# Sums, feature combinations, squares and low halves moved from GpSimd to VectorE in a two-layer diffusion transformer

## The chip, the cores and the metric

The kernel runs on one core of a Trainium2 chip. The metric is the device time of one execution in microseconds (us); the time shown for the kernel before is the median of three runs. Five engines work side by side: TensorE (PE in the profile, with PEld for its weight loads), VectorE (DVE), ScalarE (ACT), GpSimd (POOL) and SyncE (SP), which issues the transfers here.

## The reference, cut to what matters

Two layers run over 1024 latent tokens and 256 context tokens of width 1024. Layer 0 mixes by dense grouped attention and a pooling mixer, layer 1 by windowed attention. Around every mixer and every feed-forward block stand an RMS norm, a modulation from a conditioning vector, and a second norm on the way out:

```python
mod = (silu_c @ w_mod[l] + b_mod[l])[:, None, :]
sh_m, sc_m, gt_m, sh_f, sc_f, gt_f = jnp.split(mod, 6, axis=-1)
h = rmsnorm(x, g_pre_mix[l]) * (1 + sc_m) + sh_m
x = x + gt_m * rmsnorm(mixer(h), g_post_mix[l])
h = rmsnorm(x, g_pre_ffn[l]) * (1 + sc_f) + sh_f
g, u = jnp.split(h @ w_in, 2, axis=-1)
x = x + gt_f * rmsnorm((silu(g) * u) @ w_out, g_post_ffn[l])
```

The context goes through the same with its own modulation, in layer 0 only.

## The kernel before, in words

**Precision by halves.** Matrix products are made in a 32-bit format that TensorE takes in one pass. To keep accuracy, each operand is split: ScalarE copies it to that format (the high half, names with `wh`, `hh`, `th`, `ph`), and a subtraction leaves the low half (`wl`, `hl`, `tl`, `pl`). `split` does this for activations and `wunit` for a 128x1024 piece of weights. A product is then three matmuls. The variable `wpool[0]` says how many of the 1024 columns of a weight's low half GpSimd makes; VectorE makes the rest. It is set from the constants `WP0` to `WP7`, `OUTWP0` and `OUTWP` stage by stage, and to all 1024 columns inside `pair_up`, for the units of the gate weights that are kept for later.

**Tiles.** The tokens are held with features on the partitions, in chunks of 512 latent tokens (`l0`, `l1`) and 256 context tokens (`cc`). Large tiles come from a ring of 38 buffers (`Q`), half-size ones from a ring of 19 (`S`), modulation weights from a ring of 3 (`MW`), and results of matmuls from 8 banks (`ps`).

**Norms.** `rstd` squares eight feature rows on ScalarE and adds the squares in two accumulators; before the change the first is added on VectorE and the second on GpSimd. VectorE then adds the two, TensorE sums over the partitions, ScalarE takes the root, VectorE the reciprocal, and TensorE spreads it over the partitions again. `postnorm` scales the block's output and adds it to the stream (feature rows 1, 3 and 5 of that addition on GpSimd, the others on VectorE); `prenorm` makes the split input of the next product.

**Modulation.** `mod_row` makes two of layer 0's six vectors by matmul. `mod_vec` makes the others by multiply-and-add over eight 128-row pieces of the weights: an addend with number `(k + 2c) % 4` below `pool` is scaled on ScalarE (`S_mp`) and added on GpSimd, the others are one instruction on VectorE (`S_ma`). Layer 0's vectors 2, 3 and 4 are called with `POOLC`, which is 4 before, so that all their sums go to GpSimd; the rest of the vectors use VectorE alone.

**Feed-forward by a fast product.** The gate product of chunk `l0` is made ahead of time (`ffn_gates`) while attention runs, and chunk `l1` follows in `ffn_pair` by a two-by-two fast matrix product that needs sums and differences of inputs and weights. `pair_up` leads into it: output projection's `postnorm`, `rstd`, the last kept gate units, and `prenorm_pair`, which makes for each of four feature rows four combinations of the two chunks (`S_t`) and splits five (`Q_th`, `Q_tl`). For each of the 22 units of weights, `ffn_pair` makes four combinations of weight columns (`Q_sw`), splits them (`Q_wh`, `Q_wl`; `S_wh`, `S_wl`), runs the products, adds their results (`S_v`), multiplies by the gate (`S_v` again) and splits the result (`S_act`), which goes to memory. `ffn_out` multiplies that by the output weights.

**Who sets the order.** Nothing runs as it is written. `Plan` records every instruction, gives it a cost by a table, and `layout` places the instructions by list scheduling: per engine, the ready one with the lowest priority number, subject to free buffers and to a rule that VectorE and GpSimd do not run instructions on on-chip operands at one time (`port_free`). Each engine then works through its fixed list in order. All instructions are issued from line 419, so the profile's groups are told apart by the tiles' names.

Quoted, `wunit`'s division of a low half:

```python
c = D - wpool[0]
if c:
    V.tensor_tensor(wl[:, :c], raw[:, :c], r32(wh[:, :c]), op=ALU.subtract)
if c < D:
    G.tensor_tensor(wl[:, c:], raw[:, c:], r32(wh[:, c:]), op=ALU.subtract)
```

Of the kernel before, what the change touches and what calls it, by code (L numbers as in the profile page):

```python
# [32 lines left out]
MODLATE = (2, 3, 4)  # L33
POOLE = 4
OUTM = ("0", "c")
OUTWP0 = 1024
OUTWP = 500
OUTL = False
TAILX = (1, 3, 5, 7)
WP0 = 200  # L40
WP1 = 0
WP2 = 200
WP3 = 500
WP4 = 340
WP5 = 0
WP6 = 0
REST = 1.0
WP7 = 600
SIZES = (2, 4, 4, 4, 4, 4), (2, 4, 4, 4, 4, 4), (4, 4, 4, 4, 6)
EARLY = 2  # L50
PSPL = True
POOLC = 4
SHARES = (0.9, 0.95, 0.9, 0.7)
KEPT = (5, 2), (7, 3)
POOLX = (1, 3, 5)
# [371 lines left out]
def tile_dit(  # L427
# [92 lines left out]
    def split(hi, lo, src, pool=False):  # L520
        S.activation(hi, src, AF.Copy)
        (G if pool else V).tensor_tensor(lo, src, r32(hi), op=ALU.subtract)
# [15 lines left out]
    def rstd(xf):  # L538
        n = xf.ch.n
        kk, nt = 512 // n, n // P  # L540
        accs = [None, None]
        for k in range(0, KT, kk):
            sq = st([P, kk, n], F32, "sq")
            for j in range(kk):
                S.activation(sq[:, j, :], xf.k(k + j), AF.Square)
            i = k // kk % 2
            if accs[i] is None:
                accs[i] = sq
            else:
                (G if i else V).tensor_tensor(accs[i], accs[i], sq, op=ALU.add)  # L550
        acc, other = accs
        V.tensor_tensor(acc, acc, other, op=ALU.add)
        acc = acc[:, 0, :]
        if kk > 1:
            V.tensor_tensor(acc, acc, accs[0][:, 1, :], op=ALU.add)
        ps = pst(2 * nt)
        for t in range(nt):
            T.matmul(ps[:, 2 * t:2 * t + 2], acc[:, t * P:(t + 1) * P], ones2, start=True, stop=True)
        r = small([P, 4], F32, "rs")[:, :nt]
        S.activation(r, ps[:, 0:2 * nt:2], AF.Sqrt, bias=epsc, scale=1.0 / D)  # L560
        V.reciprocal(r, r)
        rb = st([P, 4, P], F32, "rb")[:, :nt, :]
        V.tensor_copy(rb, r.unsqueeze(2).to_broadcast([P, nt, P]))
        pr = pst(n)
        for t in range(nt):
            T.transpose(pr[:, t * P:(t + 1) * P], rb[:, t, :], ident)
        return pr
# [18 lines left out]
    def prenorm_pair(xf, r, x0, l, kind):  # L586

        a = fin[:, l, 2 * kind, 0, :]  # L590
        b = mod[:, l, 3 * kind, 0, :]
        db = small([P, 4], F32, "db")
        V.tensor_tensor(db, b[:, 4:8], b[:, 0:4], op=ALU.subtract)
        for k in range(KT):
            V.scalar_tensor_tensor(xf.k(k), xf.k(k), a[:, k:k + 1], r, op0=ALU.mult, op1=ALU.mult)
        t = [(Quad("th"), Quad("tl")) for _ in range(5)]
        for k in range(4):
            lo1, hi1, lo0, hi0 = xf.k(k), xf.k(k + 4), st([P, 512], F32, "x0"), st([P, 512], F32, "x0")
            SP.dma_start(out=lo0, in_=x0[:, k, :])
            SP.dma_start(out=hi0, in_=x0[:, k + 4, :])  # L600
            bk = b[:, k + 4:k + 5]
            t1, t2, t3, t4 = (st([P, 512], F32, "t") for _ in range(4))
            G.tensor_tensor(t1, lo1, lo0, op=ALU.subtract)
            V.scalar_tensor_tensor(t2, hi1, bk, t1, op0=ALU.add, op1=ALU.subtract)
            V.scalar_tensor_tensor(t3, hi1, db[:, k:k + 1], lo1, op0=ALU.add, op1=ALU.subtract)
            V.scalar_tensor_tensor(t4, hi0, bk, t2, op0=ALU.add, op1=ALU.subtract)
            for i, f in ((1, t2), (2, t3), (0, t1), (3, t4)):
                split(t[i][0].k(k), t[i][1].k(k), f, i in (0, 2))
            S.activation(t[4][0].k(k), hi1, AF.Identity, bias=bk, scale=1.0)
            V.scalar_tensor_tensor(t[4][1].k(k), hi1, bk, r32(t[4][0].k(k)), op0=ALU.add, op1=ALU.subtract)  # L610
        return t
# [165 lines left out]
    def ffn_pair(l, t, first, hc=None):  # L777
# [3 lines left out]
        for u in range(NH):  # L781
# [5 lines left out]
            gs = qt_([P, 2, 512], F32, "gs")  # L787
            SP.dma_start(out=gs, in_=g_scr[l][:, u, :, :])
            p1, p2 = (qt_([P, 2, 512], F32, "sw") for _ in range(2))
            G.tensor_tensor(p1[:, 0, :], up[:, 0:512], up[:, 512:1024], op=ALU.add)  # L790
            G.tensor_tensor(p1[:, 1, :], p1[:, 0, :], ga[:, 0:512], op=ALU.subtract)
            G.tensor_tensor(p2[:, 0, :], ga[:, 0:512], up[:, 0:512], op=ALU.subtract)
            G.tensor_tensor(p2[:, 1, :], ga[:, 512:1024], p1[:, 1, :], op=ALU.subtract)
            s12, s34 = [(qt_([P, 2, 512], F32R, "wh"), qt_([P, 2, 512], F32R, "wl")) for _ in range(2)]
            a22 = st([P, 512], F32R, "wh"), st([P, 512], F32R, "wl")
            split(*s12, p1)
# [17 lines left out]
            def late(u=u, gs=gs, s34=s34, p5=p5, v2=v2, uu=uu, cu=cu, cg=cg, prod=prod):  # L814
                prod(p5, s34, 1, b22, False, True)
                V.tensor_tensor(cg, v2, p5, op=ALU.add)
                for ch, g, v in ((L0, gs[:, 1, :], uu), (L1, cg, cu)):
                    S.activation(g, g, AF.Silu)
                    G.tensor_tensor(v, v, g, op=ALU.mult)
                    hi, lo = st([P, 512], F32R, "act"), st([P, 512], F32R, "act")  # L820
                    split(hi, lo, v)
                    for j, o in enumerate((hi, lo)):
                        SP.dma_start(out=a_scr[l][ch][:, u, j, :], in_=r32(o))
# [736 lines left out]
```

## Time and profile before

| what | value |
|---|---|
| median of three runs | 2852.52 us (2847.48 to 2853.18) |
| the profiled execution's own time | 2850.01 us |
| its span, first to last instruction | 2848.1 us |
| mean granted TensorE clock | 0.968 |
| bytes moved | 481.08 MB, mean 169 GB/s |

The stages lie in the span about as follows: start and first projections to 100 us; layer 0's attention, pooling mixer and later modulation vectors to 400; output projections and the way into the second attention to 550; attention of `l1` with gates of `l0` to 800; the way into the pair to 900; the pair's units to 1250; output weights to 1450; the way into layer 1 to 1550; layer 1's attention, with the rest of layer 0's feed-forward and then with gates, to 2150; output projection and the way into the second pair to 2310; its units to 2600; the last output weights to the end.

To read a row of stretches: the stretch and its length, then for each engine its busy microseconds with the count of instructions, then the mean granted clock, the busy share of the transfer engines and the bytes per second. A row of a timeline has start, length, engine, instruction and count, and in brackets how long the engine stood idle before it and for whom. The ends of matmuls are modelled, so 512-column matmuls of 0.39 us overlap one another.

### The profile page before, as it was taken

The numbers are of one execution on the slowest core, as the hardware profiler recorded it, in microseconds if no ns is written. First come the engines' busy times: TensorE is split into PE (matmuls) and PEld (weight loads), VectorE is DVE, ScalarE is ACT, GpSimd is POOL, SyncE is SP. The second block draws the span as 40 slices with busy tenths as digits, with TensorE's granted clock in tenths as the row PEclk, the third lists the DMA queues.
The fourth block names the chain that finished last, engine by engine and source line by source line (L and its number), as shares of the span: only waits on it lengthen the run. The fifth ranks groups of instructions, "written<-read, shape, count | busy, mean of one in ns | idle before, by whom it ended". The sixth has DMA issues, their size and how long they took to land. (4 is left out here: it accounts for less than half of the span.)

```text
span 2848.1 us, 39713 instructions
## 1 busy us (share of the span) xinstructions
PE 2674.4 (94%) x13781; PEld 2206.7 (77%) x13781; DVE 1922.8 (68%) x3292; ACT 1399.4 (49%) x2896; POOL 1035.0 (36%) x764
## 2 busy tenths in 40 slices
PE   8989898899998999999989998998999989999998
PEld 4766677688886788788877877877878768888887
DVE  4677776766457998875465478787883597762334
ACT  4579875565553333331143357687775533333011
POOL 1475755000045555430032512534002677651002
PEclk9999999999998999999999998998999999999999
DMA  7333456333563655676534643444335435556442
GB/s 282 116 108 125 142 195 226 131 117 119 176 225 112 224 204 210 240 276 244 204 111 129 218 128 125 135 143 154 111 101 211 170 133 192 199 182 220 168 177 75
DMA packets 240905, 481.08 MB, mean 169 GB/s; under 512 B 24128, under 2 KB 85824, under 8 KB 240704
## 3 DMA queue, kind: packets, MB, share of 16 engines
q1 hardware_dynamic: 240704, 478.54, 48.6%
q8 instruction: 109, 1.79, 0.3%
q14 instruction: 92, 0.75, 0.1%
HBM read 350.52 MB, written 123.99 MB: 167 GB/s over the span
## 5 line engine op out<-in xcount | busy, mean ns | idle before, releaser
L419 PE MATMUL ps<-Q_ac,Q_wh 128*128 128x512 f32 (+1 forms) x1920 | 534.0, 360 | 5.8 <-ACT Q_wh L419 3.0
L419 PEld LDWEIGHTS ps<-Q_ac,Q_wh 128*128 128x128 f32 x1920 | 344.7, 192 | 56.0 <-ACT Q_wh L419 4.0
L419 PE MATMUL ps<-Q_hh,Q_wh 128*128 128x512 f32 (+1 forms) x992 | 364.4, 377 | 13.7 <-ACT Q_hh L419 5.7
L419 PE MATMUL ps<-Q_hl,Q_wh 128*128 128x512 f32 (+1 forms) x992 | 362.4, 374 | 2.2 <-DVE Q_hl L419 2.1
L419 ACT ACTIVATE Q_wh<-Q_raw 128x1024 fp32r<-128x1024 f32 x202 | 213.0, 1061 | 294.0 <-DMA Q_raw<-in_w_ffn_out 113.2
L419 PE MATMUL ps<-Q_ac,Q_wl 128*128 128x512 f32 (+1 forms) x960 | 344.4, 360 | 8.9 <-DVE Q_wl L419 5.6
L419 POOL TENSOR_TENSOR Q_wl<-Q_raw,Q_wh 128x500 fp32r<-128x500 f32 (+4 forms) x121 | 187.3, 1558 | 359.1 <-ACT Q_wh L419 285.1
L419 DVE TENSOR_TENSOR Q_wl<-Q_raw,Q_wh 128x1024 fp32r<-128x1024 f32 (+4 forms) x182 | 198.0, 1097 | 149.0 <-ACT Q_wh L419 121.0
L419 PE MATMUL ps<-Q_th,Q_wh 128*128 128x512 f32 x704 | 279.8, 400 | 18.6 <-ACT Q_th L419 12.7
L419 PE MATMUL ps<-Q_tl,Q_wh 128*128 128x512 f32 x704 | 278.7, 397 | 1.0 <-DVE Q_tl L419 0.5
L419 PE MATMUL ps<-Q_kt,S_q 128*128 128x256 f32 (+3 forms) x992 | 255.7, 341 | 23.5 <-ACT Q_p L419 12.3
L419 DVE TENSOR_TENSOR S_pl<-ps,S_ph 128x512 fp32r<-128x512 f32 (+1 forms) x328 | 213.1, 671 | 78.3 <-ACT S_ph L419 72.1
L419 POOL TENSOR_TENSOR S_sq<-S_sq,S_sq 128x512 f32<-128x512 f32 x48 | 68.3, 1424 | 543.7 <-ACT S_sq L419 537.0
L419 PE MATMUL ps<-Q_hh,Q_wl 128*128 128x512 f32 (+1 forms) x992 | 263.7, 371 | 0.0
L419 DVE TENSOR_TENSOR Q_yf<-Q_yf,ps 128x512 f32<-128x512 f32 (+1 forms) x200 | 117.0, 588 | 210.1 <-PE ps L419 209.3
L419 ACT ACTIVATE S_ph<-ps 128x512 fp32r<-128x512 f32 (+1 forms) x328 | 185.4, 608 | 85.3 <-PE ps L419 81.9
L419 PEld LDWEIGHTS ps<-Q_hh,Q_wh 128*128 128x128 f32 x992 | 189.9, 192 | 45.1 <-ACT Q_hh L419 11.4
L419 PEld LDWEIGHTS ps<-Q_hl,Q_wh 128*128 128x128 f32 x992 | 190.2, 192 | 30.3 <-DVE Q_hl L419 4.0
L419 PEld LDWEIGHTS ps<-Q_kt,S_q 128*128 128x128 f32 x992 | 171.1, 195 | 54.5 <-ACT Q_p L419 18.3
L419 PEld LDWEIGHTS ps<-Q_ac,Q_wl 128*128 128x128 f32 x960 | 183.9, 192 | 36.4 <-DVE Q_wl L419 7.9
L419 PEld LDWEIGHTS ps<-Q_hh,Q_wl 128*128 128x128 f32 x992 | 175.3, 191 | 28.5 <-issue 0.9
L419 PE MATMUL ps<-Q_th,Q_wl 128*128 128x512 f32 x704 | 190.5, 392 | 6.6 <-DVE Q_wl L419 6.6
(196 smaller groups left out, 6028.8 us busy)
## 6 DMA issues: line engine op xcount, KB each, us to landing
Q_raw<-in_w_ffn_in SPq DMA_DIRECT2D x132, 512.0 KB, 4.5
a_scr_l<-S_act SPq DMA_DIRECT2D x176, 256.0 KB, 2.0
Q_ac<-a_scr_l SPq DMA_DIRECT2D x88, 512.0 KB, 6.5
mw<-in_w_mod SPq DMA_DIRECT2D x160, 256.0 KB, 3.6
Q_raw<-in_w_ffn_out SPq DMA_DIRECT2D x66, 512.0 KB, 8.1
S_q<-q_scr_l SPq DMA_DIRECT2D x192, 128.0 KB, 3.5
g_scr<-S_gs SPq DMA_DIRECT2D x88, 256.0 KB, 2.0
Q_gs<-g_scr SPq DMA_DIRECT2D x44, 512.0 KB, 5.6
```

What stands on the lines that cost most here:

```text
L419: getattr(eng.real, op)(*args, **kw)
```

## The change

It does four things. The constants of `wunit` go to zero, so that VectorE makes all columns of the weights' low halves (except for `pair_up`, which sets its own value and is not touched). The second accumulator of `rstd`, the four weight combinations and two gate products of each unit of `ffn_pair`, and one combination and two splits of each feature row in `prenorm_pair` go from GpSimd to VectorE. `POOLC` goes from 4 to 2, so that half of the addends of layer 0's vectors 2 to 4 become single instructions on VectorE instead of a copy on ScalarE and an addition on GpSimd. The scheduler then makes a new order.

```diff
-OUTWP0 = 1024
-OUTWP = 500
+OUTWP0 = 0
+OUTWP = 0
...
-WP0 = 200
+WP0 = 0
 WP1 = 0
-WP2 = 200
-WP3 = 500
-WP4 = 340
+WP2 = 0
+WP3 = 0
+WP4 = 0
...
-WP7 = 600
+WP7 = 0
...
-POOLC = 4
+POOLC = 2
...
-                (G if i else V).tensor_tensor(accs[i], accs[i], sq, op=ALU.add)
+                V.tensor_tensor(accs[i], accs[i], sq, op=ALU.add)
...
-            G.tensor_tensor(t1, lo1, lo0, op=ALU.subtract)
+            V.tensor_tensor(t1, lo1, lo0, op=ALU.subtract)
...
-                split(t[i][0].k(k), t[i][1].k(k), f, i in (0, 2))
+                split(t[i][0].k(k), t[i][1].k(k), f)
...
-            G.tensor_tensor(p1[:, 0, :], up[:, 0:512], up[:, 512:1024], op=ALU.add)
-            G.tensor_tensor(p1[:, 1, :], p1[:, 0, :], ga[:, 0:512], op=ALU.subtract)
-            G.tensor_tensor(p2[:, 0, :], ga[:, 0:512], up[:, 0:512], op=ALU.subtract)
-            G.tensor_tensor(p2[:, 1, :], ga[:, 512:1024], p1[:, 1, :], op=ALU.subtract)
+            V.tensor_tensor(p1[:, 0, :], up[:, 0:512], up[:, 512:1024], op=ALU.add)
+            V.tensor_tensor(p1[:, 1, :], p1[:, 0, :], ga[:, 0:512], op=ALU.subtract)
+            V.tensor_tensor(p2[:, 0, :], ga[:, 0:512], up[:, 0:512], op=ALU.subtract)
+            V.tensor_tensor(p2[:, 1, :], ga[:, 512:1024], p1[:, 1, :], op=ALU.subtract)
...
-                    G.tensor_tensor(v, v, g, op=ALU.mult)
+                    V.tensor_tensor(v, v, g, op=ALU.mult)
```

VectorE's list on the way into layer 0's pair, before: the third feature row's combinations (`S_t_2068`, `S_t_2070`, their low halves `Q_tl_2040` and `Q_tl_2048`) stand among modulation sums (`S_ma`) and the context's first unit (`S_gc`, `S_wl`).

```order
L419 SCALAR_TENSOR_TENSOR S_ma_2928<-mw_2934,c_75,S_ma_2928 128x512
L419 SCALAR_TENSOR_TENSOR S_ma_2927<-mw_2935,c_75,S_ma_2927 128x512
L419 TENSOR_TENSOR S_wl_2151<-Q_raw_2142,S_wh_2150 128x512
L419 SCALAR_TENSOR_TENSOR S_ma_2928<-mw_2935,c_75,S_ma_2928 128x512
L419 TENSOR_TENSOR S_gc_2138<-S_gc_2138,ps_2139 128x256
L419 TENSOR_TENSOR S_act_2140<-S_gc_2138,S_act_2140 128x256
L419 SCALAR_TENSOR_TENSOR S_t_2068<-Q_x_1992,mod,S_t_2067 128x512
L419 SCALAR_TENSOR_TENSOR S_ma_2927<-mw_2936,c_75,S_ma_2927 128x512
L419 SCALAR_TENSOR_TENSOR S_t_2070<-S_x_2066,mod,S_t_2068 128x512
L419 TENSOR_TENSOR Q_tl_2040<-S_t_2068,Q_th_2038 128x512
L419 SCALAR_TENSOR_TENSOR S_ma_2928<-mw_2936,c_75,S_ma_2928 128x512
L419 TENSOR_TENSOR Q_tl_2048<-S_t_2070,Q_th_2046 128x512
```

The same place now: the last feature row's nine instructions, and behind them the first unit's first weight combination (`Q_sw_2048`).

```order
L419 TENSOR_TENSOR Q_tl_2006<-S_t_2028,Q_th_2004 128x512
L419 SCALAR_TENSOR_TENSOR Q_tl_2010<-Q_x_1950,mod,Q_th_2008 128x512
L419 TENSOR_TENSOR S_t_2031<-Q_x_1948,S_x_2029 128x512
L419 SCALAR_TENSOR_TENSOR S_t_2033<-Q_x_1950,db_1990,Q_x_1948 128x512
L419 SCALAR_TENSOR_TENSOR S_t_2032<-Q_x_1950,mod,S_t_2031 128x512
L419 TENSOR_TENSOR Q_tl_1994<-S_t_2031,Q_th_1992 128x512
L419 SCALAR_TENSOR_TENSOR S_t_2034<-S_x_2030,mod,S_t_2032 128x512
L419 TENSOR_TENSOR Q_tl_1998<-S_t_2032,Q_th_1996 128x512
L419 TENSOR_TENSOR Q_tl_2002<-S_t_2033,Q_th_2000 128x512
L419 TENSOR_TENSOR Q_tl_2006<-S_t_2034,Q_th_2004 128x512
L419 SCALAR_TENSOR_TENSOR Q_tl_2010<-Q_x_1950,mod,Q_th_2008 128x512
L419 TENSOR_TENSOR Q_sw_2048<-Q_raw_2046 128x512
```

All four feature rows, 36 instructions, now stand in one run, and the modulation sums behind them.

GpSimd's list on the way into layer 1's pair, before: the last of seven full-width low halves of kept gate weights (`Q_wl`), the last square of the output's norm (`S_sq`), and the additions to the stream (`Q_x`).

```order
L419 TENSOR_TENSOR Q_wl_4955<-Q_raw_4953,Q_wh_4954 128x1024
L419 TENSOR_TENSOR Q_wl_4958<-Q_raw_4956,Q_wh_4957 128x1024
L419 TENSOR_TENSOR S_sq_4964<-S_sq_4964,S_sq_4970 128x512
L419 TENSOR_TENSOR Q_x_4959<-Q_x_4959,Q_y_4906 128x512
L419 TENSOR_TENSOR Q_x_4960<-Q_x_4960,Q_y_4915 128x512
```

The same place now (the numbers of the names differ between the two programs):

```order
L419 TENSOR_TENSOR Q_wl_4913<-Q_raw_4911,Q_wh_4912 128x1024
L419 TENSOR_TENSOR Q_wl_4916<-Q_raw_4914,Q_wh_4915 128x1024
L419 TENSOR_TENSOR Q_x_4917<-Q_x_4917,Q_y_4864 128x512
L419 TENSOR_TENSOR Q_x_4918<-Q_x_4918,Q_y_4873 128x512
L419 TENSOR_TENSOR Q_x_4919<-Q_x_4919,Q_y_4882 128x512
```

The seven low halves stay on GpSimd; the square behind them has left for VectorE's list.

## The prediction

> **What bounds the kernel now.** I read the page's first part, then stretches cut at the stages, then the timeline where TensorE stands idle.
>
> ```profile
> PE 2674.4 (94%) x13781; PEld 2206.7 (77%) x13781; DVE 1922.8 (68%) x3292; ACT 1399.4 (49%) x2896; POOL 1035.0 (36%) x764
> ```
> ```profile
> 100.00:400.00 300.00, 270.52 (x1360) 203.12 (x1360) 229.12 (x409) 244.91 (x553) 199.38 (x200) 0.96 0.46 149
> 450.00:550.00 100.00, 76.47 (x428) 65.33 (x427) 86.97 (x144) 63.52 (x134) 31.31 (x19) 0.88 0.45 157
> 850.00:900.00 50.00, 36.65 (x188) 30.48 (x187) 38.09 (x48) 16.46 (x29) 22.65 (x15) 0.80 0.32 117
> 900.00:1250.00 350.00, 338.22 (x1683) 284.33 (x1682) 308.83 (x362) 124.32 (x197) 189.95 (x121) 0.99 0.61 214
> 1450.00:1550.00 100.00, 85.48 (x395) 68.45 (x395) 68.38 (x113) 42.17 (x74) 39.47 (x28) 0.91 0.34 116
> 1700.00:2150.00 450.00, 417.04 (x2500) 355.85 (x2499) 372.43 (x1010) 336.68 (x901) 121.17 (x90) 0.95 0.39 125
> 2225.00:2310.00 85.00, 68.90 (x277) 52.99 (x276) 64.33 (x68) 40.40 (x62) 57.95 (x36) 0.88 0.40 146
> 2310.00:2600.00 290.00, 289.26 (x1275) 238.82 (x1274) 206.12 (x211) 108.42 (x148) 186.28 (x121) 1.00 0.57 203
> ```
>
> TensorE is the bound: 94% busy, so 2848.1 - 2674.4 = 174 us of idle are all that faster helpers can give back, and besides them the time that its clock is lowered around an idle spell (0.80 in 850 to 900). Where GpSimd has most to do, in the pairs' units (186 of 290 us from 2310 on), TensorE waits for 0.7 us only. The idle time lies at the passages between stages (23.5, 13.4, 14.5 and 16.1 us in the rows from 450, 850, 1450 and 2225) and in the attentions (29.5 from 100, 33 from 1700). So nearly all of the moved work is hidden today; the change is worth what it does at the passages and in the attentions.
>
> **What moves, and its price.** What leaves GpSimd:
>
> ```profile
> L419 POOL TENSOR_TENSOR Q_wl<-Q_raw,Q_wh 128x500 fp32r<-128x500 f32 (+4 forms) x121 | 187.3, 1558 | 359.1 <-ACT Q_wh L419 285.1 <-PE ps L419 65.9 <-issue 6.5
> L419 POOL TENSOR_TENSOR Q_tl<-S_t,Q_th 128x512 fp32r<-128x512 f32 x16 | 24.8, 1552 | 20.0 <-ACT Q_th L419 19.9
> L419 POOL TENSOR_TENSOR S_t<-Q_x,S_x 128x512 f32<-128x512 f32 x8 | 12.4, 1563 | 22.8 <-DMA mw<-in_w_mod 12.6 <-DVE Q_x L419 6.6 <-DMA Q_raw<-in_w_ffn_in 1.8
> ```
> The stretch over the whole span with the combinations alone (first) and with the `S_v` alone (second); GpSimd's column is the last busy one:
> ```profile
> 0.00:2848.10 2848.10, 130.68 (x88) 92.73 (x88) 272.16 (x176) 0.97 0.49 169
> 0.00:2848.10 2848.10, 245.49 (x308) 82.77 (x132) 140.15 (x88) 0.97 0.49 169
> ```
> Minimum, median and maximum of the same addition on both engines, of a VectorE split that runs beside GpSimd's work, and of both kinds of modulation sum:
> ```profile
> L419 DVE TENSOR_TENSOR S_sq<-S_sq,S_sq x74: 652/691/2876, 9.3 to 2835.4; 128x512 f32<-128x512 f32 x74
> L419 POOL TENSOR_TENSOR S_sq<-S_sq,S_sq x48: 1262/1298/2330, 9.8 to 2834.1; 128x512 f32<-128x512 f32 x48
> L419 DVE TENSOR_TENSOR S_act<-S_v,S_act x88: 675/1152/1797, 904.6 to 2593.8; 128x512 fp32r<-128x512 f32 x88
> L419 DVE SCALAR_TENSOR_TENSOR S_ma<-mw,c,S_ma x140: 734/744/1876, 486.9 to 1399.5; 128x512 f32<-128x512 f32 x140
> L419 POOL TENSOR_TENSOR S_ma<-S_ma,S_mp x84: 1266/1286/2890, 138.2 to 385.0; 128x512 f32<-128x512 f32 x84
> ```
>
> VectorE takes on 176 + 88 + 48 + 24 = 336 additions of 512 columns at 0.69 us, 232 us; 42 of the 84 modulation sums and six first addends at 0.74 at most, 36 us; and of the weights' columns, by the constants, 16 x 200 + 8 x 1024 in layer 0 and 28 x 500 + 23 x 340 + 12 x 200 + 22 x 600 later, 48,800 at 0.69/512 us, 66 us. Together 334 us on top of 1923. What comes back is contention: a `S_act` split takes 0.675 us at the least and 1.797 at the most, 1.12 more, nearly one GpSimd addition (1.26). Its median is 0.48 above the least, so 88 of them return about 42 us.
>
> The SBUF page of the Trainium skill ("Who interferes with whom") says that a VectorE instruction with two on-chip inputs and a GpSimd one that reads there block each other for the whole instruction; the 1.12 against 1.26 agrees. By that rule the pairs' stages get back about what they take on; by the idle of 0.7 us after 2310 it is worth nothing there either way.
>
> In the units from 900 to 1250 VectorE is busy 309 of 350 us already, with those waits in it. Six additions a unit (4.1 us) come, and splits shorten; I take no change, covered by the waits that go. If the cover is gone, the 11.8 us of idle there grow first.
>
> **Layer 1's passage, -14.** The next timelines are of ScalarE, GpSimd, VectorE and TensorE here:
>
> ```profile
> 2223.86 0.63 ACT L419 ACTIVATE S_sq<-Q_y 128x512 f32<-128x512 f32 x1
> ...
> 2218.74 17.07 POOL L419 TENSOR_TENSOR Q_wl<-Q_raw,Q_wh 128x1024 fp32r<-128x1024 f32 x7 [2.75 <-PE ps L419]
> 2235.77 1.29 POOL L419 TENSOR_TENSOR S_sq<-S_sq,S_sq 128x512 f32<-128x512 f32 x1
> ...
> 2237.09 0.69 DVE L419 TENSOR_TENSOR S_sq<-S_sq,S_sq 128x512 f32<-128x512 f32 x1 [15.42 <-POOL S_sq L419]
> 2249.37 3.42 DVE L419 TENSOR_TENSOR Q_x<-Q_x,Q_y 128x512 f32<-128x512 f32 x2
> 2252.71 4.88 DVE L419 TENSOR_TENSOR S_sq<-S_sq,S_sq 128x512 f32<-128x512 f32 x4
> 2265.22 5.34 DVE L419 SCALAR_TENSOR_TENSOR Q_x<-Q_x,fin,ps 128x512 f32<-128x512 f32 x8
> 2298.98 3.49 DVE L419 TENSOR_TENSOR Q_tl<-S_t,Q_th 128x512 fp32r<-128x512 f32 x2
> ...
> 2263.50 0.60 PE L419 MATMUL ps<-ident,S_rb 128*128 128x128 f32 x4
> ```
>
> The last square is ready at 2224.5 but queues behind seven weight splits on GpSimd until 2235.8: on VectorE its two additions end near 2226, 11 us early. The seven splits stay on GpSimd, though, and the stream's three additions there now wait for their end; that and blocked VectorE additions give back some 3. The adds of 3.42 and 4.88 us shrink by about 3 in all. From the end of the eight `Q_x` (2270.6) to the last `Q_tl` (2302.5) it takes 32 us; now it is 36 instructions in one run at 5.34/8 = 0.67 us, 24: 8 earlier. In all 19 to 22 us earlier, so the last feature row is split near 2281, and the first weights about 2 later. TensorE is out of gates at 2263.5. At the rate after 2310 (1275/290 = 4.4 matmuls per us), 277 matmuls are 63 us of 85, so 22 are lost here; of the new gap of 18 to 20 some 11 are filled by products with rows that are ready, as now. Lost then 8: -14.
>
> **Layer 0's passage, -12.**
> ```profile
> 838.13 5.36 DVE L419 SCALAR_TENSOR_TENSOR Q_x<-Q_x,fin,ps 128x512 f32<-128x512 f32 x8 [0.25 <-PE ps L419]
> ...
> 888.97 0.68 DVE L419 TENSOR_TENSOR Q_tl<-S_t,Q_th 128x512 fp32r<-128x512 f32 x1
> ```
> From 843.5 to 889.6 it is 46 us, with modulation sums between. One run of 36 is 24. The four combinations and four splits of the first unit follow (some 6 us), so it can start near 874, where now the last `Q_tl` alone ends at 889.6: 16 us. Idle (13.4) and clock (a fifth of 36.7, 7) cost 20 there; I take 12. The modulation sums wait behind the run, and with three `MW` buffers the loads queued on SP behind theirs do too: 6 of the 12 could be lost again.
>
> **The way into the second attention, -10.** GpSimd, then VectorE:
> ```profile
> 450.34 10.11 POOL L419 TENSOR_TENSOR Q_wl<-Q_raw,Q_wh 128x1024 fp32r<-128x1024 f32 x4
> ...
> 450.44 2.88 DVE L419 TENSOR_TENSOR S_sq<-S_sq,S_sq 128x512 f32<-128x512 f32 x1 [8.46 <-POOL S_sq L419]
> 466.32 9.64 DVE L419 TENSOR_TENSOR Q_x<-Q_x,Q_y 128x512 f32<-128x512 f32 x5
> ```
> VectorE waits 8.5 us for a square queued behind weight splits, then takes 2.88 for an add of 0.69 and 9.64 for five of 3.5: 8.5 + 2.2 + 6.1 = 17 us. Its new load on this path, some of the eight splits (1.4 each) and six squares, is 5 to 8. Of the 9 to 12 us gained I take 10; the lowered clock (0.88) is a margin.
>
> **The way into layer 1, -5; the end, -1; attentions, +4.**
> ```profile
> 1464.99 3.39 DVE L419 TENSOR_TENSOR Q_x<-Q_x,Q_yf 128x512 f32<-128x512 f32 x2
> 1475.94 5.33 DVE L419 TENSOR_TENSOR Q_x<-Q_x,Q_yf 128x256 f32<-128x256 f32 x5
> ```
> Without GpSimd's squares and splits these adds fall to about 1.4 and 2: 5 us off that path, about a third of the 14.5 idle there. The last norm's last square costs 0.69 in place of 1.30. In the attentions VectorE gains load (next part); I take 4 us as the likely part, between nothing and 62.
>
> Sum: -14 - 12 - 10 - 5 - 1 + 4 = -38. Against the profiled execution, 2850.0 - 38 = 2812 us; that execution lies 2.5 below the median, within the runs' spread (5.7 us), so 0.2% is about what a measurement can tell from no change.
>
> **The rivals.** *VectorE becomes the bound in the attentions: slower.* It is busy 372 of 450 us from 1700 on, mostly with results of matmuls, where GpSimd does not hold it up. It takes on there 28 x 500 and about 12 x 340 columns (24 us), and 36 us of modulation sums with some 2 of weights from 100 to 400, where it has 229 of 300. If all 62 show on the path, 2850 - 42 + 62 = 2870. It decides once more than 42 of the 62 become idle of TensorE. For it: the rows of both stretches show idle TensorE beside the busiest VectorE outside the pair. Against: the scheduler places this load where VectorE is free. The Trainium skill's Perfetto Trace Analysis page ("Optimizing Scalar/DVE Operations") holds that a saturated VectorE may be relieved through GpSimd, which speaks against the change, and adds that their shared port may undo it.
>
> *The attention gains too: 2790.* Half the modulation addends need no copy on ScalarE, which has 245 of 300 us from 100 to 400:
> ```profile
> L419 ACT ACTIVATE S_mp<-mw,c 128x512 f32<-128x512 f32 x84 | 57.7, 727 | 3.8 <-POOL S_ma L419 3.6
> ```
> 42 x 0.727 = 30 us. If half of the 29.5 us idle goes, and the 11.8 from 900 to 1250, 4 comes off in place of being added: 2812 - 4 - 14 - 4 = 2790.
>
> *The passages stay as they are.* Another wait, for the old chunk's rows or a buffer of the ring of 19, ends last, and -42 becomes -4: 2846.
>
> **How the numbers follow.** Forecast (2797 to 2832) 0.55; attention too 0.18; passages stay 0.11; slower 0.16. The range takes in the attention's gain down to 2778 and the slower case up to 2858. Faster by over 0.2% (below 2847): 0.55 + 0.18 + 0.05 = 0.78; within: 0.06; slower: 0.16.
>
> **What would show it.** Right: no `S_sq` of VectorE waits for GpSimd, 36 instructions in about 24 us at both pairs, `S_act` near 0.68, GpSimd near 300 us busy, and idle from 2225 to 2310 of half of 16. Wrong: TensorE's idle in the attentions above 75 us, or waits at the passages that name transfers.

## The result, and the profile after

| kernel | median us | ratio to before, 95% interval |
|---|---|---|
| before, run beside it (4 runs) | 2851.88 (2847.48 to 2853.18) | 1 |
| after (4 runs) | 2750.93 (2747.63 to 2751.25) | 0.9646 (0.9629 to 0.9663) |

The change saves 101 us, 3.5%, where 38 were forecast and the range ended at 2778. The first part of the page of after:

```profile
PE 2637.9 (96%) x13781; PEld 2186.7 (80%) x13781; DVE 1996.6 (73%) x3684; ACT 1361.9 (50%) x2846; POOL 319.5 (12%) x277
```

GpSimd lost 1035.0 - 319.5 = 715.5 us of work, and VectorE's busy time rose by only 1996.6 - 1922.8 = 74 us, though it does 392 more instructions. TensorE's idle time fell from 174 to 2745.8 - 2637.9 = 108 us. The rest is that TensorE's busy time for the same 13781 matmuls fell by 36.5 us, at a mean clock of 0.983 in place of 0.968. The same stages of after, which lie earlier in its span (columns as in the rows of before: busy us of TensorE, its weight loads, VectorE, ScalarE and GpSimd with counts, then granted clock, transfer share, GB/s):

```profile
100.00:400.00 300.00, 272.29 (x1410) 207.61 (x1409) 263.86 (x471) 223.22 (x513) 137.58 (x145) 0.99 0.48 155
450.00:550.00 100.00, 88.79 (x495) 74.59 (x493) 88.73 (x167) 67.07 (x149) 5.21 (x5) 0.90 0.42 147
800.00:850.00 50.00, 48.80 (x287) 42.94 (x286) 48.72 (x79) 29.09 (x53) 1.63 (x1) 1.00 0.64 222
850.00:1200.00 350.00, 350.00 (x1800) 298.81 (x1799) 322.20 (x517) 130.34 (x206) 0.00 (x0) 1.00 0.67 227
1400.00:1500.00 100.00, 93.87 (x441) 77.25 (x440) 70.03 (x117) 39.54 (x70) 11.84 (x11) 0.93 0.39 123
1600.00:2100.00 500.00, 471.54 (x2817) 400.88 (x2816) 414.81 (x1095) 367.18 (x977) 50.58 (x40) 0.97 0.41 132
2125.00:2200.00 75.00, 70.02 (x300) 54.47 (x299) 57.81 (x83) 38.72 (x64) 23.01 (x10) 0.98 0.48 176
```

In each of these stages TensorE waits a smaller share of the time. Its idle time went from 23.5 to 11.2 us on the way into the second attention, from 13.4 to 1.2 ahead of layer 0's pair (and its clock from 0.80 to 1.00), from 11.8 to nothing in that pair's units, from 14.5 to 6.1 on the way into layer 1, from 16.1 to 5.0 ahead of layer 1's pair. In the units VectorE is busy 322 of 350 us and TensorE waits for nothing; before it was busy 309 and TensorE waited 11.8. So a busy share can mean two things: before, part of it was VectorE held up inside its instructions. Minimum, median and maximum of three forms of VectorE in after; the first two read both operands from on-chip memory, the third reads one of them from a bank of matmul results:

```profile
L419 DVE TENSOR_TENSOR S_act<-S_v,S_act x88: 675/685/701, 859.4 to 2488.2; 128x512 fp32r<-128x512 f32 x88
L419 DVE TENSOR_TENSOR S_wl<-Q_raw,S_wh x66: 675/685/697, 841.2 to 2465.6; 128x512 fp32r<-128x512 f32 x66
L419 DVE TENSOR_TENSOR S_v<-S_v,ps x176: 672/681/694, 848.4 to 2485.4; 128x512 f32<-128x512 f32 x176
```
The last two in before:
```profile
L419 DVE TENSOR_TENSOR S_wl<-Q_raw,S_wh x66: 673/1209/1807, 856.3 to 2568.8; 128x512 fp32r<-128x512 f32 x66
L419 DVE TENSOR_TENSOR S_v<-S_v,ps x176: 670/680/690, 899.7 to 2589.9; 128x512 f32<-128x512 f32 x176
```

`S_wl` had a median of 1.21 us beside GpSimd and has 0.69 alone; `S_v<-S_v,ps`, in the same units at the same time, was never slowed at all. For all forms that both kernels have, take the fall of the mean duration times the count of before: it adds up to 185 us, and forms with a result bank as an operand account for none of it.

Where the 101 us were won can be read from TensorE, which does 13781 matmuls in both kernels: the table has the start of the matmul behind the first 1800, 2500 and so on, in the two profiled executions. Equal counts are not quite the same matmuls in the two orders, and an order alone moves a row by some us (below).

| matmuls before it | stage that ends there | before, us | after, us | ahead by | won in the stage |
|---|---|---|---|---|---|
| 1800 | start, layer 0's attention | 414.1 | 403.5 | 10.6 | 10.6 |
| 2500 | way into the second attention | 565.9 | 542.7 | 23.2 | 12.6 |
| 4100 | second attention | 851.0 | 827.0 | 24.0 | 0.8 |
| 4550 | way into layer 0's pair | 962.7 | 913.7 | 49.0 | 25.0 |
| 6100 | its units | 1275.6 | 1214.3 | 61.3 | 12.3 |
| 7500 | output weights, way into layer 1 | 1549.8 | 1479.8 | 70.0 | 8.7 |
| 11000 | layer 1's attention | 2212.8 | 2124.5 | 88.3 | 18.3 |
| 11400 | way into layer 1's pair | 2327.0 | 2222.5 | 104.5 | 16.2 |
| 13700 | its units, output weights | 2824.0 | 2722.3 | 101.7 | -2.8 |

Not all of it is idle time. From 100 to 400 TensorE idles 29.5 us before and 27.7 after; what changes more is the granted clock, 0.96 and 0.99.

Layer 1's passage of after, ScalarE, GpSimd and then VectorE:

```profile
2135.52 0.63 ACT L419 ACTIVATE S_sq<-Q_y 128x512 f32<-128x512 f32 x1
```
```profile
2130.45 18.14 POOL L419 TENSOR_TENSOR Q_wl<-Q_raw,Q_wh 128x1024 fp32r<-128x1024 f32 x7 [247.09 <-PE ps L419]
```
```profile
2136.18 5.28 DVE L419 TENSOR_TENSOR S_sq<-S_sq,S_sq 128x512 f32<-128x512 f32 x2 [2.79 <-ACT S_sq L419]
...
2150.11 1.41 DVE L419 SCALAR_TENSOR_TENSOR Q_y<-Q_y,fin,ps 128x512 f32<-128x512 f32 x2 [6.13 <-PE ps L419]
...
2171.75 0.69 DVE L419 TENSOR_TENSOR S_t<-Q_x,S_x 128x512 f32<-128x512 f32 x1
...
2193.92 0.74 DVE L419 SCALAR_TENSOR_TENSOR Q_tl<-Q_x,mod,Q_th 128x512 fp32r<-128x512 f32 x1
```

The squares no longer queue behind the seven weight splits, but two of them take 5.28 us beside those splits; then VectorE waits 6.13 us for the spread of the norm, which stands in TensorE's queue behind gate products; and the feature rows are one run of 36 instructions, 2171.8 to 2194.7, 22.9 us.

### The profile page after: what moved, and what is told of

Its sections match the earlier page's. It is cut to its first block, busy times and chain, and to the rows that moved or that the text cites. A ratio compares the mean times of both kernels' runs of the same rounds, so it can differ in the third digit from the quotient of the medians.

```text
span 2745.8 us, 39261 instructions
## 1 busy us (share of the span) xinstructions
PE 2637.9 (96%) x13781; PEld 2186.7 (80%) x13781; DVE 1996.6 (73%) x3684; ACT 1361.9 (50%) x2846; POOL 319.5 (12%) x277
## 4 chain that ended last, share of the span: by engine, by line
PE 71%; DVE 11%; ACT 4%; DMA 3%; issue 2%; POOL 1%; SPq 0%; DVEq 0%; ACTq 0%; POOLq 0%
PE ps L419 71%; DVE Q_x L419 1%; DVE S_fw L419 1%; DVE ps L419 1%; DVE mx L419 1%; ACT S_ph L419 1%; DVE Q_hl L419 1%; ACT Q_p L419 1%; DVE Q_yf L419 1%; DVE S_sq L419 1%; DMA Q_raw<-in_wo_in 1%; DVE Q_tl L419 1%; ACT S_p L419 1%; DVE S_pl L419 1%; DVE Q_wl L419 1%
## 5 line engine op out<-in xcount | busy, mean ns | idle before, releaser
L419 DVE TENSOR_TENSOR Q_wl<-Q_raw,Q_wh 128x1024 fp32r<-128x1024 f32 x190 | 235.3, 1248 | 137.7 <-ACT Q_wh L419 112.7
L419 ACT ACTIVATE S_ph<-ps 128x512 fp32r<-128x512 f32 (+1 forms) x328 | 186.0, 604 | 88.3 <-PE ps L419 84.8
L419 PEld LDWEIGHTS ps<-Q_kt,S_q 128*128 128x128 f32 x992 | 171.0, 195 | 47.5 <-issue 12.6
L419 PE MATMUL ps<-ident,Q_p 128*128 128x128 f32 x928 | 185.3, 277 | 10.6 <-DVE S_pl L419 3.1
L419 ACT ACTIVATE Q_p<-ps,nb 128x256 f32<-128x256 f32 (+1 forms) x336 | 185.3, 562 | 15.1 <-DVE nb L419 14.7
```

Source lines behind the costliest of these rows:

```text
L419: getattr(eng.real, op)(*args, **kw)
```

## The experiments

Theory 1: a GpSimd addition holds up every VectorE instruction with two on-chip operands for about its own length, so an addition moved to VectorE costs VectorE itself little, and every chain gets shorter. Theory 2: only waits in GpSimd's queue at the passages counted. Theory 3: the planner's new order was lucky.

**Each part alone, in the kernel before** (2849.96 us beside them).

`e1_pair`, the edits of the change in `prenorm_pair` and `ffn_pair` and nothing else; two of its seven lines:
```diff
-            G.tensor_tensor(t1, lo1, lo0, op=ALU.subtract)
+            V.tensor_tensor(t1, lo1, lo0, op=ALU.subtract)
...
-                    G.tensor_tensor(v, v, g, op=ALU.mult)
+                    V.tensor_tensor(v, v, g, op=ALU.mult)
```
`e2_squares`:
```diff
-                (G if i else V).tensor_tensor(accs[i], accs[i], sq, op=ALU.add)
+                V.tensor_tensor(accs[i], accs[i], sq, op=ALU.add)
```
`e3_weights`, the seven constants of `wunit` at 0, of which two:
```diff
-OUTWP0 = 1024
+OUTWP0 = 0
...
-WP7 = 600
+WP7 = 0
```
`e4_modsums`:
```diff
-POOLC = 4
+POOLC = 2
```


> The kernel before, with only the pair's part of the change: weight combinations, gate products, the one feature combination and the two feature splits go to VectorE. Theory 1 (a GpSimd addition blocks VectorE's additions on on-chip operands for its whole 1.3 us, so doing it on VectorE in 0.69 us is cheaper for VectorE itself, everywhere): TensorE's 11.8 us of idle in layer 0's pair units go, and of the two passages into the pairs the feature part, some 15 each: 2852 - 40 = 2812 us, and VectorE's busy time rises by less than 50 us for 200 moved additions of 0.69 us (138 us). Theory 2 (only waits in GpSimd's queue at the passages counted): the units gain nothing, the passages some 6 each: about 2840 us, VectorE's busy time up by 100 or more. Theory 3 (a lucky order): anything, without a pattern by stage.

> The kernel before, with only the second accumulator's 48 additions of squares on VectorE. Theory 1: they leave GpSimd's queue, so the waits of 15.4 us (way into layer 1's pair) and 8.5 us (way into the second attention) go, but the weight splits on GpSimd still block VectorE there: about -20, 2832 us. Theory 2 (queue waits are most of the 102 us): -50 or more, 2800 us or less. Theory 3: no pattern.

> The kernel before, with only the constants of the weights' low halves at zero, so VectorE makes them all outside the gate units kept for later. Theory 1: 48800 columns at 1.3 ns leave VectorE and GpSimd both with less, the square before the second attention no longer queues, and the adds at the passages are not blocked: about -25, 2827 us. Theory 2: only the 8.5 us wait goes: about -10, 2842 us; the 15.4 us wait behind the kept units' seven splits stays in both. Theory 3: no pattern.

> The kernel before, with only the modulation sums halved on GpSimd (42 of 84 become one instruction on VectorE). Theory 1: 42 additions of 1.29 us that block VectorE go and 42 of 0.74 come, and 30 us leave ScalarE: the first attention gains some 8 us: 2844 us. Theory 2: nothing, 2852 us. Theory 3: no pattern.

| alone | median us | saved | ratio, 95% interval |
|---|---|---|---|
| pair | 2803.91 | 46.1 | 0.9835 (0.982 to 0.985) |
| squares | 2835.39 | 14.6 | 0.9947 (0.9927 to 0.9968) |
| weights | 2826.06 | 23.9 | 0.9914 (0.9898 to 0.9931) |
| modulation sums | 2835.37 | 14.6 | 0.9947 (0.9932 to 0.9962) |

The four add up to 99 of the 101 us: no single part did it. Theory 2 expected the pair to give 10 and the squares 50; it was the other way round. The squares' row is instructive. VectorE in the kernel with the squares alone, at layer 1's passage:

```profile
2213.37 5.29 DVE L419 TENSOR_TENSOR S_sq<-S_sq,S_sq 128x512 f32<-128x512 f32 x2 [2.79 <-ACT S_sq L419]
...
2227.29 1.41 DVE L419 SCALAR_TENSOR_TENSOR Q_y<-Q_y,fin,ps 128x512 f32<-128x512 f32 x2 [6.12 <-PE ps L419]
```

The wait of 15.42 us for GpSimd's `S_sq` is gone, as theory 1 had said, but the two additions take 5.29 us beside the splits, and the wait for TensorE's queue is 6.12 us, where it was 1.59 in before. The stretch around that passage:

```profile
2200.00:2290.00 90.00, 78.22 (x302) 60.30 (x301) 64.69 (x67) 41.89 (x67) 53.79 (x30) 0.83 0.41 146
```

TensorE idles 11.8 us at a clock of 0.83, in before 16.1 at 0.88: counting the lowered clock as 0.17 x 78 = 13 and 0.12 x 69 = 8 us, 25 are lost here and 24 there. Next to nothing was won at this place (by the count of matmuls this kernel is 11.2 us ahead of before at 11000 and 12.5 at 11400). What the squares gave lies mostly on the way into layer 1, where the idle time in the same 100 us fell from 14.5 to 7.7.

**The pair's part divided, and order alone.** `e8_features` has the edits of `prenorm_pair` alone (the first line above and the two splits), `e11_units` those of `ffn_pair` alone (the second and the four combinations). `e5_replan` (in before) and `e9_replan_after` (in after) change no work:
```diff
-    LAT_DMA = 1500
+    LAT_DMA = 1600
```


> The kernel before, with only the feature rows' part of the pair on VectorE (one combination and two splits of each of four rows; the units' weight combinations and gate products stay on GpSimd). Theory 1: the two runs into the pairs get 8 us shorter each, and the units' share of the 46 us stays out: 2850 - 18 = 2832 us, with layer 0's units at their 11.8 us of idle as before. Theory 2: all of the 46 us belongs to the passages: 2805 us.

> The kernel before, with only the units' part of the pair on VectorE: four weight combinations and two gate products of each of the 44 units. Theory 1: the two parts of the pair add up, so 46 less the 10 of the feature rows: 2850 - 36 = 2814 us, with layer 0's units free of TensorE's idle time. Theory 2: the units gain only the 12 us of idle time that stood in layer 0's: 2838 us, and what is left of the 46 comes only with both.

> The kernel before, with nothing changed but one number of the planner, its guess of a transfer's latency (1600 in place of 1500 ns): the same instructions on the same engines in another order. Theory 1 (the gains are those of the work moved): within 8 us of 2850. Theory 3 (a lucky order): 15 us or more to either side, as much as the 15 us that each of the two smaller parts gave.

> The kernel after with nothing changed but the planner's guess of a transfer's latency (1600 in place of 1500 ns). If an order alone is worth some 7 us, as in the kernel before (2848.6 to 2841.7), this lies within 8 us of 2751. If the 102 us hung on a lucky order of the kernel after, a part of 20 us or more is lost here: 2770 us or more.

Features alone: 2838.29 us beside 2848.62, 10.3 saved (0.9962, 0.9950 to 0.9974). Units alone: 2821.81 beside 2850.67, 28.9 saved (0.9902, 0.9887 to 0.9916); the other 7 of the 46 came only with both, which is no more than another order can be worth (below). Layer 0's units with the features alone, then with the units alone:

```profile
900.00:1250.00 350.00, 336.18 (x1673) 282.40 (x1672) 319.63 (x367) 125.42 (x198) 193.19 (x120) 0.99 0.62 216
```
```profile
900.00:1250.00 350.00, 350.00 (x1788) 298.47 (x1788) 314.23 (x498) 135.56 (x216) 0.00 (x0) 1.00 0.70 238
```

With the combinations on GpSimd TensorE idles 13.8 us; without them it idles not at all, and VectorE, with 131 instructions more, is busy 5 us less.

Another order of the same work: 2841.70 beside 2848.62 in before (0.998, 0.997 to 0.9989), and 2752.53 in after (0.9658, 0.9644 to 0.9673), against 2750.93. An order alone is worth up to 7 us. It also shifts time between stages: in before with the other order, TensorE's idle time in the 100 us from 450 goes from 23.5 to 16.6, and the kernel is 4.9 us ahead after 4100 matmuls, but 1.3 behind after 4500, ahead of layer 0's pair; the rest is won further on. So theory 3 explains none of the four parts in full, but about half of the two parts of 14.6 would be within it. For the modulation sums that was tested (below); for the squares it stays open.

**GpSimd's additions by themselves.** `e6_adds8` adds to after, in each of the 44 units, eight additions whose result nobody reads. `d` is a tile of its own, and the planner's port rule is switched off for it. `e12_scalar` puts ScalarE's copies in their place.
```diff
+            for _ in range(8):
+                G.tensor_tensor(d, ga[:, 0:256], ga[:, 256:512], op=ALU.add)
```
```diff
+            for _ in range(8):
+                S.activation(d, ga[:, 0:256], AF.Copy)
```


> The kernel after, with eight additions of 256 columns on GpSimd in each of the 44 pair units, whose results nobody reads, and of which the planner does not know that they touch VectorE: at half of 1.29 us each some 5.5 us a unit, 240 us of GpSimd's time in all. Theory 1 (GpSimd's additions block VectorE's): VectorE's busy time rises by 100 to 200 us, the median of the activations' splits leaves 0.69, and layer 0's units, where VectorE has 1.3 us to spare a unit, get 1 to 4 us longer each: 2751 + 25 to 90 us. Theory 2 (only what waited in GpSimd's queue was paid): nothing waits for these additions, so the time stays within 5 us of 2751 and VectorE's busy time at 1997.

> The control of the 82 us that the eight unread additions cost: the same eight per unit as copies of 256 columns on ScalarE, reading the same weights and so holding the same buffers. If GpSimd's additions cost by blocking VectorE: within 8 us of 2751 and VectorE's busy time at 1997. If they cost by holding the weights' buffers or by the order that the planner made around them: 2800 us or more, like them.

With the additions 2833.54 us (0.9953, 0.9938 to 0.9968), 82.6 more than after. With the copies 2753.36 (0.9654, 0.9638 to 0.9670), 2.4 more. So neither the order nor the mere holding of the weights cost, but GpSimd's reading beside VectorE. The copies let the weights go sooner (0.42 us each against 1.07 in the median), but held buffers can be only a small part: all that waits for the additions in their trace is ScalarE's `Q_wh`, 6.4 us in all, and VectorE once, 0.3 us. The additions' own row, GpSimd and VectorE side by side in a unit, then both pages' first parts, of the additions and of the copies:

```profile
L419 POOL TENSOR_TENSOR du<-Q_raw x352: 731/1068/2931, 819.0 to 2550.1; 128x256 f32<-128x256 f32 x176
```
```profile
1176.53 8.46 POOL L419 TENSOR_TENSOR du<-Q_raw 128x256 f32<-128x256 f32 x8 [9.23 <-DMA Q_raw<-in_w_ffn_in]
```
```profile
1179.03 0.74 DVE L419 TENSOR_TENSOR Q_sw<-Q_raw 128x512 f32<-128x512 f32 x1 [0.41 <-DMA Q_raw<-in_w_ffn_in]
1179.69 0.68 DVE L419 TENSOR_TENSOR S_v<-S_v,ps 128x512 f32<-128x512 f32 x1
1180.29 0.68 DVE L419 TENSOR_TENSOR Q_sw<-Q_sw,Q_raw 128x512 f32<-128x512 f32 x1
1180.89 1.22 DVE L419 TENSOR_TENSOR Q_sw<-Q_raw,Q_raw 128x512 f32<-128x512 f32 x1
1182.04 1.23 DVE L419 TENSOR_TENSOR S_v<-S_v,S_v 128x512 f32<-128x512 f32 x1
1183.19 1.21 DVE L419 TENSOR_TENSOR Q_sw<-Q_raw,Q_sw 128x512 f32<-128x512 f32 x1
1184.33 1.21 DVE L419 SCALAR_TENSOR_TENSOR S_ma<-mw,c,S_ma 128x512 f32<-128x512 f32 x1
1185.46 0.68 DVE L419 TENSOR_TENSOR S_act<-S_v,S_act 128x512 fp32r<-128x512 f32 x1
1186.06 0.67 DVE L419 TENSOR_TENSOR S_v<-S_v,ps 128x512 f32<-128x512 f32 x1
```
```profile
PE 2659.8 (94%) x13781; PEld 2192.9 (77%) x13781; DVE 2103.0 (74%) x3684; ACT 1367.7 (48%) x2846; POOL 703.0 (25%) x629
```
```profile
PE 2642.8 (96%) x13781; PEld 2188.8 (79%) x13781; DVE 1994.3 (72%) x3684; ACT 1485.7 (54%) x3198; POOL 319.5 (12%) x277
```

GpSimd's run lasts to 1185.0. Four instructions of VectorE in it take 1.21 to 1.23 us in place of 0.68 (0.74 for the modulation sum), one after the other; once it is over they take 0.68 again. It isn't every one: the two combinations at the top took 0.74 and 0.68, and the median of `S_act` stays at 0.68, where 1 was expected, since the eight additions run in a bunch as the weights land. GpSimd is held too: 0.73 us at the least, 1.07 in the median. VectorE's busy time rises by 106 us for the same 3684 instructions, and 83 show in the time. The SBUF page of the Trainium skill ("Who interferes with whom") says that an instruction of VectorE with two inputs in SBUF, the on-chip memory outside the result banks, contends with a GpSimd one that reads there, and one with at most one such input doesn't, outside VectorE's two-port modes. The rows agree on both counts: 1.22 us for the first kind, 0.68 for the `S_v<-S_v,ps` inside the run, and at most 0.69 for all 176 of these:

```profile
L419 DVE TENSOR_TENSOR S_v<-S_v,ps x176: 668/674/689, 859.5 to 2571.5; 128x512 f32<-128x512 f32 x176
```

One input tensor alone does not make a form safe, though. The first addends of the modulation sums (`S_ma<-mw,c`, 20 in before) take 0.48 us in the median there, but up to 2.62 and 0.81 in the mean; in after the mean is 0.52.

**The first attention.** `e10_sums_back` is after with `POOLC = 4`; `e13_copies` has that too, but adds on VectorE; `e14_all_sums` is after with `POOLC = 0`.
```diff
-                            G.tensor_tensor(a, a, t, op=ALU.add)
+                            V.tensor_tensor(a, a, t, op=ALU.add)
```


> The kernel after, with the modulation sums of layer 0's later vectors all on GpSimd again. Theory 1, if the 15 us that this part gave alone are its own: 2765 us, lost in layer 0's attention or just behind it. If most of those 15 us were the new order on the way into the second attention (the other replanned kernel lost 10 us less there too): within 6 us of 2751.

> The kernel after, with all 84 modulation addends copied on ScalarE again as in the kernel before, but added on VectorE and not on GpSimd. Against the kernel whose sums went back to GpSimd (2763 us), only the engine of the additions differs; against the kernel after, ScalarE has 30 us more and VectorE some 30. If the 13 us of the first attention are GpSimd's additions blocking VectorE: within 6 us of 2751. If they are ScalarE's copies, ahead of the exponentials that TensorE waits for: 2763 us or more.

> The kernel after, with the other half of the modulation addends as single instructions on VectorE too, none on ScalarE or GpSimd. If either cause holds, the second half should give about as much as the first: 2751 - 10 = 2741 us. If VectorE becomes the bound in the first attention (264 of 300 us busy, 31 more to come): 2755 to 2770 us.

Sums back: 2763.36 us (0.9698, 0.9683 to 0.9712), 12.4 lost, so the part's 14.6 were mostly its own. With copies on ScalarE and additions on VectorE 2753.26 (0.9668, 0.9653 to 0.9682), 10.1 less. All sums on VectorE: 2744.39 (0.9635, 0.9617 to 0.9654), another 8.9 less and the fastest of all kernels here, though its interval overlaps that of after. The first step changes only the engine of the 84 additions; the second takes 96 copies off ScalarE (84 addends and 12 first ones) and gives VectorE 12 instructions more. So both GpSimd's additions and ScalarE's copies cost, about alike. After itself lies between, with half of the copies and half of GpSimd's additions, so that its nearness to the second kernel does not clear the copies. Each step is only a little more than an order can be worth. The stretch of the attention in the three:

```profile
100.00:400.00 300.00, 266.50 (x1350) 202.59 (x1348) 227.07 (x406) 241.87 (x548) 189.10 (x187) 0.96 0.46 148
```
```profile
100.00:400.00 300.00, 271.25 (x1390) 208.88 (x1389) 274.30 (x501) 249.47 (x559) 88.24 (x104) 0.96 0.47 150
```
```profile
100.00:400.00 300.00, 278.37 (x1440) 213.35 (x1439) 286.64 (x524) 198.00 (x470) 84.87 (x104) 0.99 0.48 155
```

TensorE gets through 1350, 1390 and 1440 matmuls in these 300 us (1410 in after). In the third VectorE is busy 287 of 300 us, and TensorE still waits less than in the other two.

**How far it goes.** `e7_more` is after with `wpool[0] = 0` in `pair_up` and `POOLX = ()`; `e16_kept` has the first edit alone, `e17_stream` the second; `e15_rotary` is `e14_all_sums` with the rotary products and `PSPL`'s splits on VectorE.
```diff
-        wpool[0] = D
+        wpool[0] = 0
...
-POOLX = (1, 3, 5)
+POOLX = ()
```


> The kernel after, with the twelve weight splits of the units kept for the two pairs and the feature rows of the stream's additions (39) on VectorE too. Theory 1: 30 + 43 us leave GpSimd; the two squares that took 5.28 us beside the seven splits of layer 1's pair take 1.3, and the stream's last two additions are not held: some 5 off each of the passages: 2740 us. Theory 2: no wait in GpSimd's queue is left there, so nothing: 2751 us. VectorE as the bound: seven splits of 1.25 us stand ahead of the squares, 9 us more: 2760 us.

> The kernel after, with only the twelve kept units' weight splits on VectorE (half of the edit that lost 12 us). If they are what loses, standing ahead of the squares on VectorE: 2758 us or more, at both passages. If the stream's additions are: within 6 us of 2751.

> The kernel after, with only the stream's additions (feature rows 1, 3 and 5) on VectorE, the other half of the edit that lost 12 us. If GpSimd helps there, because VectorE has matmul results to scale meanwhile and nothing it could be blocked in: 2758 us or more. If blocking costs there too: 2745 us.

> The kernel with all modulation sums on VectorE (2744 us), with the rotary products and the query, pooling and mixer splits of the attentions on VectorE too (some 120 instructions, 150 us of GpSimd). If GpSimd's additions cost wherever VectorE has work: 2744 - 10 = 2734 us. If VectorE, with 287 of 300 us busy in the first attention, becomes the bound there: 2755 us or more.

Both edits: 2763.30 us (0.9706, 0.9692 to 0.9720), 12.4 more than after, against theory 1. The kept units' splits alone: 2751.18 (0.9640, 0.9619 to 0.9661), nothing. The stream's additions alone: 2765.44 (0.9699, 0.9684 to 0.9713), all of the loss. VectorE there, in the kernel with the stream's additions moved, then in after, and GpSimd in after:

```profile
2168.21 1.29 DVE L419 TENSOR_TENSOR Q_x<-Q_x,Q_y 128x512 f32<-128x512 f32 x2
2169.42 1.40 DVE L419 SCALAR_TENSOR_TENSOR Q_y<-Q_y,fin,ps 128x512 f32<-128x512 f32 x2
```
```profile
2151.43 0.69 DVE L419 TENSOR_TENSOR Q_x<-Q_x,Q_y 128x512 f32<-128x512 f32 x1
2152.03 1.40 DVE L419 SCALAR_TENSOR_TENSOR Q_y<-Q_y,fin,ps 128x512 f32<-128x512 f32 x2
```
```profile
2151.59 1.68 POOL L419 TENSOR_TENSOR Q_x<-Q_x,Q_y 128x512 f32<-128x512 f32 x1 [3.00 <-DVE Q_y L419]
```

Here GpSimd's addition of 1.68 us lies beside two VectorE instructions that read a result bank, 1.40 us, and holds up nobody; on VectorE it costs 0.60 on the path of the norm. The 39 such additions (15 of 512 columns, 24 of 256, at some 0.60 and 0.34) are 17 us, and 14.5 were lost. In after, 35 of the 43 us of these additions lie beside VectorE instructions with a result bank as an operand. By the count of matmuls only some 2 us are lost at this place, 4 to 5 ahead of layer 0's pair, where the rows are of the same kind, and 8 in layer 1's attention, where the rows were not compared.

With the rotary products and splits moved as well, 2757.45 (0.9670, 0.9655 to 0.9684), some 13 more than without: VectorE, 290 of 300 us busy in the first attention, is at its limit there, or those products too lay beside matmul results. The two were not tested apart. By the count of matmuls some 7 us are lost in the first attention and 9 in layer 1's, where VectorE is busy 425 of 500 us, so the limit of the first attention is not all of it.

## Why the prediction was wrong in size

The mechanism, GpSimd's additions holding VectorE's, was named rightly and priced far too low, and the sum set the units at nothing and the attentions at a loss.

**The contention that comes back: 42 us forecast, 185 measured. This step failed first.** It was worked out from `S_act` alone, 88 instructions. `S_act` did give 39. But `S_wl` gave 35, the splits of the combinations 25, the modulation sums 16, and many smaller forms the rest: the row of one form was taken for the whole engine. Of the 334 us of new work VectorE's busy time shows 74. (The lengths of its instructions add up to 125 us more; instructions in a row overlap in the profile, 0.60 us apart at 0.68 each, so the busy time shows less.)

**"I take no change" in the pair's units: 12 us won in the profile.** The units' edits alone save 28.9 us, of which some 14 lie in layer 0's units and 10 on the way into them. The prediction had the row that pointed there, 309 busy of 350 us "with those waits in it", and the rule of the SBUF page of the Trainium skill beside it, and still set the waits that go against the new work as equal. They are not: by the units' rows VectorE did 131 instructions more in 5 us less. So the 11.8 us of idle there, which the sum only thought of as growing, went.

**Layer 0's passage, -12.** Right place, undersized: the prediction counted 20 us lost there and took 12, with no row for the 8 that it left. Idle went from 13.4 to 1.2 us and the clock from 0.80 to 1.00, so nearly all of the 20 came; by the count of matmuls 25 were won, the first units' part included.

**Attentions, +4, and the slower rival's up to +62: wrong sign, and the largest miss of the sum.** By the count of matmuls 10.6 us were won to the end of the first attention and 18.3 in layer 1's. In the first, the modulation sums are worth 12.4, and with all of them VectorE was busy 287 of 300 us without TensorE waiting more. In layer 1's, the weights' low halves alone, which were to cost up to 24 us there, put the kernel 10 us further ahead (16.0 after 7500 matmuls, 25.8 after 10500), of which another order could give about 4; what they freed there was not traced further. The prediction argued that the moved work is hidden because TensorE does not wait where GpSimd has most to do, in the pairs' units (186 of 290 us). But its own row of the first attention has 199 of 300, a larger share, with TensorE idle 29.5 us. Nor was the pair the only place where VectorE was busier than in the attentions: the row from 450 has 87 of 100.

The second rival, 2790, had the sign, and its reason, ScalarE's copies, is about half of what the first attention's sums gave. Its sum names the 11.8 us from 900 to 1250 but leaves them out; with them it is 2778, still too slow. The Perfetto Trace Analysis page of the Trainium skill ("Optimizing Scalar/DVE Operations"), which the prediction set against the change, grants that a saturated VectorE may give work to GpSimd, and adds that it might not help. Here the second holds for additions beside VectorE's own, and the first for additions beside matmul results.

**Layer 1's passage, -14: about right, by a wrong path.** Idle fell from 16.1 to 5.0 us, and the run of 36 took 22.9 us for a forecast of 24. But the squares were to end 11 us earlier. Counted from ScalarE's last square they end 5.3 us after it (2136.15 to 2141.46) in place of 13.3 (2224.49 to 2237.78), 8 earlier, and 6.13 - 1.59 = 4.5 of that go to TensorE's queue; alone they gave next to nothing there. The wait of 1.59 in before:

```profile
2242.29 1.41 DVE L419 SCALAR_TENSOR_TENSOR Q_y<-Q_y,fin,ps 128x512 f32<-128x512 f32 x2 [1.59 <-PE ps L419]
```

The pair's part gave most of the gain: alone it put the kernel 12 us further ahead here, of 16.2 in all. So the size came out right partly by luck.

**The ways into the second attention (-10), into layer 1 (-5), and the end (-1).** Idle went from 23.5 to 11.2 and from 14.5 to 6.1; the terms were of the right size, a little low (12.6 and 8.7 by the count of matmuls). How much each edit did there is not settled, since another order alone took 6.9 us of idle off the first. In the last 245 us TensorE idles 14.1, as in the last 248 of before (13.2): the -1 didn't show.

**The clock.** The sum counts a lowered clock only ahead of layer 0's pair, 7 us. Of the 102 us by which the profiled spans differ, 66 are idle time of TensorE and 36.5 its busy time, which fell as the mean granted clock rose from 0.968 to 0.983.

Of the five signs named in advance, four came true as written (no `S_sq` of VectorE waits for GpSimd, the runs of 36 in 22.8 and 22.9 us, `S_act` at 0.685, GpSimd at 319.5 us busy); the fifth, half of 16 us idle at layer 1's passage, was too cautious at 5.0. The forecast of 2797 to 2832 and the range to 2778 missed 2751 mostly by the attentions, the units and layer 0's passage: the sum had +4, nothing and -12 for them, and 29, 12 and 25 us were won.

## What to carry to other kernels

When VectorE and GpSimd both work on on-chip operands, compare minimum and mean of VectorE's forms, all forms and not one. The median misses it: the 88 splits of the combinations had a minimum of 1.21 us, a median of 1.22 and a mean of 1.49 in before. Count times the gap, summed, was 306 us in before and 120 in after, where GpSimd still works 320 us. So the first sum is too high for what the move gives back (185 here), but one form (40) is far too low. Moving work to VectorE then costs it that much less than its price. In these runs GpSimd's additions were best left where they ran beside VectorE instructions that read matmul results, and moving more helped only up to a point: the last products moved, with VectorE 290 of 300 us busy in one stage, cost 13 us. Move one part at a time, and replan once without any change, to know what an order alone is worth.

## What was not expected of the hardware

The hold-up is mutual: eight additions of 256 columns beside VectorE made instructions of 0.68 us take 1.21 to 1.23, and took 1.07 us each in the median in place of 0.73 at the least. The additions of matmul results, `S_v<-S_v,ps`, with one operand from a result bank, kept their 0.67 to 0.69 us through all of it.
